# Writing the diagonal blocks of the linear attention's weights into its matrix by one masked copy

## The chip, the cores and the metric

The kernel runs on one core of one Trainium2 chip. The metric is the device time of the program in microseconds (us); lower is better. Its engines are TensorE (PE, matrix products; its weight loads have their own row, PEld), VectorE (DVE), ScalarE (ACT), GpSimd (POOL) and SyncE (SP), each with a queue of its own that it works off in order.

## What is computed

A network of two blocks over 256 tokens and a context of 256. The first block is run for two layers, the second for two. The change touches one branch of the first block, the gated linear attention, in both of its layers and in both directions of time. Its core in the reference, cut:

```python
GLA_HEADS, GLA_DK, GLA_DV, GLA_CHUNK = 4, 64, 128, 64

def gla_scan(q, k, v, g, s0):
    mask = jnp.tril(jnp.ones((GLA_CHUNK, GLA_CHUNK), dtype=bool))
    def step(s, inp):
        qc, kc, vc, gc = inp
        b = jnp.cumsum(gc, axis=2)
        b_last = b[:, :, -1:, :]
        inter = jnp.einsum('bhtd,bhde->bhte', qc * jnp.exp(b), s)
        rel = jnp.where(mask[:, :, None], b[:, :, :, None, :] - b[:, :, None, :, :], -jnp.inf)
        att = jnp.einsum('bhtd,bhsd,bhtsd->bhts', qc, kc, jnp.exp(rel))
        o = inter + jnp.einsum('bhts,bhse->bhte', att, vc)
        s_new = jnp.exp(b_last[:, :, 0, :])[..., None] * s + \
            jnp.einsum('bhsd,bhse->bhde', kc * jnp.exp(b_last - b), vc)
        return s_new, o
    ...
    y_gla = gla_finish(ol_f + flip(ol_b), p['gla_o_norm'], x.dtype) * jax.nn.silu(g_g)
```

`att` is the matrix of weights: for a pair of positions s and t the product of key and query with a decay per channel, exp(b_t - b_s). `o` is `att` times the values plus what the state `s` of earlier chunks gives. The scan runs forward and backward in time, over the context and then over the tokens, and the branch is the sum of both directions.

## The kernel before

`first_block` runs `trunk(0)` for 512 positions (context and tokens, four tiles of 128) and `trunk(1)` for the 256 tokens (two tiles). In each, `gla(l, hp)` is called for two pairs of heads, so the loop over `self.tiles` at L947 has 4 + 4 + 2 + 2 = 12 turns; a turn is called a tile below. Forward and backward channels of a head share the 128 partitions (0 to 63 and 64 to 127), so one product with all of them gives the sum of both directions.

A tile's matrix `att` (128 x 128 for each of two heads) is built by levels, because exp(b_t - b_s) does not factor safely over long distances. At level `lev` a pair of positions in neighbouring blocks of size B = 2^lev is taken by way of the border between them: `e` is the distance of the summed decay `cv` from the border (L972), Abs and Exp on ACT (L974, L975), `qe = e * q` (L977, DVE), half of it set to zero by POOL (L982, L983), `e * k` (L984), and then products of `e` and `qe`. Levels 5 and 6 (blocks of 32 and 64) go straight to their places in the PSUM tile `pa` (L996). Levels 0 to 4 lie inside diagonal blocks of 32; `blocks` (L958) computes for each the four 32x32 diagonal blocks of both heads into `pc[:, lev]` (8 products, L962), 128 partitions x 2 x 32. The plain product of keys and queries (s = t, no decay) goes to `pc[:, 5]`. DVE copies `pc[:, 5]` to `blk` (L999) and puts each level in with `copy_predicated` under a mask of the pairs that belong to it (L1002, five times).

The diagonal blocks of `pa` get products of zeros (`self.zero`, L1006), ACT copies `pa` to `att` (L1007), and the output `po` of each head sums S times `ec` (the state's part, L1014), `att` times `v` (L1015) and, for the diagonal blocks, `blk` times `v` in four products on 32 x 32 parts of the array (L1018). Products of the helper `mm` carry its line, L218, in the trace. In the trace a product of f32 operands shows as two records, and PSUM tiles of this part are called px, those of the big products pg.

Around it: the same PE queue carries the big products of the other branches with weights streamed from memory. `weight` (L237) loads a 512 KB piece by SP's queue (`raw`, three buffers), ACT writes its rounded part `wh` (L214) and DVE the rest `wl` (L215); products then run in three passes (`mm3`). `trunk` steps generators (`units`) for the other branches between the stages of `gla` by fixed paces. The order on each engine is set by the framework's scheduler, which places instructions by its own estimates and by priorities (`urgent`), so an edit in one line can move others. At the end of layer 1, `out_ln` loads rows by POOL's queue: `nwrow`, `wab` (L1238) and two rows into the buffer of `m` (L1068, L1069), which must wait until that buffer's last readers are done.

Of the kernel before, what the change touches and what calls it, by code (L numbers as in the profile page):

```python
# [11 lines left out]
U8 = mybir.dt.uint8  # L12
# [5 lines left out]
P = 128  # L18
# [14 lines left out]
def plan():  # L33
# [9 lines left out]
    for l in range(2):  # L43
# [31 lines left out]
        att()  # L75
        sgu()
        gla(0)
        branch("bs", M_S)
        gate(A_G)
        gla(1)  # L80
        branch("ba", M_A)
        gate(G_G)
# [98 lines left out]
class Builder:  # L181
# [144 lines left out]
    def build(self):  # L326
        nc, tc, io = self.nc, self.tc, self.io
        self.filler = iter(())
        with tc.tile_pool(name="const", bufs=1) as cp, \
# [19 lines left out]
            self.U1, self.L1, self.ones = (con[:, i * P:(i + 1) * P] for i in range(3))  # L349
            self.id32 = con[:, 3 * P:]  # L350
            self.maskc = cp.tile([P, 5, 2, 32], U8, name="maskc")
            self.mask = cp.tile([P, 5, 32], U8, name="mask")

            self.pick = cp.tile([P, 35], F32, name="pick")
            nc.vector.memset(self.pick, 0.0)
            nc.vector.memset(self.pick[:, 2:3], 1.0)
            self.zero = self.pick[:, 3:35]
            self.cols = cp.tile([P, NCOL], F32, name="cols")
            self.rope = cp.tile([P, 2, 2, 64], F32, name="rope")
            self.eps = cp.tile([P, 1], F32, name="eps")  # L360
# [484 lines left out]
    def gla(self, l, hp):  # L845

        nc, tc, io = self.nc, self.tc, self.io
        T0, TN = self.T0, self.TN
        nt = len(self.tiles)
        with tc.tile_pool(name=f"gla{l}{hp}", bufs=1, reuse_waits="tile") as gp:  # L850
# [13 lines left out]
            v = self.t(gp, [P, 4, 256], tag="v")  # L864
# [4 lines left out]
            q = self.t(gp, [P, 2, TN], tag="q")  # L869
# [24 lines left out]
            for i2 in range(2):  # L894
                pc = self.ps()
                for h in range(2):
                    for i in range(2):
                        o = (h * 2 + i) * P
# [14 lines left out]
            for i2 in range(2):  # L913
# [7 lines left out]
                for i in range(2):  # L921
                    for h in range(2):
                        o = (i * 2 + h) * P
# [4 lines left out]
                for i in range(2):  # L928
                    for h in range(2):
                        o = (i * 2 + h) * P  # L930
                        self.mm(pu[:, o:o + P], kt[:, o:o + P], v[:, 2 * i2 + i, h * P:(h + 1) * P], True, True)
                nc.scalar.copy(up[:, 2 * i2:2 * i2 + 2].rearrange("p a b c -> p (a b c)"), pu)
            for (rows, order) in ((slice(0, 64), (0, 1, 2, 3)), (slice(64, 128), (1, 0, 3, 2))):
                nc.gpsimd.memset(S[rows, order[0]], 0.0)
                nc.scalar.copy(S[rows, order[1]], up[rows, order[0]])
                for n in (1, 2):
                    i, nx = order[n], order[n + 1]
# [9 lines left out]
            for n, i in enumerate(self.tiles):  # L947
                tt = i * P - T0
                cv = c[:, :, i * P:(i + 1) * P]
                qv = q[:, :, tt:tt + P]  # L950
                kv = kd[:, :, i * P:(i + 1) * P]

                att = self.t(gp, [P, 2, P], tag="att", bufs=2)
                blk = self.t(gp, [P, 2, 32], tag="blk", bufs=2)
                pc = self.ps()[:, :384].rearrange("p (l a t) -> p l a t", l=6, a=2)
                pa = self.ps()[:, :256].rearrange("p (a t) -> p a t", a=2)

                def blocks(out, x, y):  # L958
                    for a in range(2):
                        for b in range(4):  # L960
                            o = slice(32 * b, 32 * b + 32)
                            nc.tensor.matmul(out[o, a, :], x[:, a, o], y[:, a, o], start=True, stop=True, tile_position=(0, 32 * b))  # L962

                blocks(pc[:, 5], kv, qv)
                for levs in (range(0, 4), range(4, 7)):
                    nl = len(levs)
                    e = self.t(gp, [P, nl, 2, P], tag="e", bufs=2)
# [17 lines left out]
                    for li, lev in enumerate(levs):  # L985
# [5 lines left out]
                        for a in range(2):  # L991
                            for m in range(P // (2 * B)):
                                for d in range(2):
# [2 lines left out]
                                    nc.tensor.matmul(pa[ks, a, ts], e[ch, li, a, ks], qe[ch, li, a, ts], start=True, stop=True,  # L996
                                                     tile_position=(64 * d, s0))
                    if levs[0] == 0:
                        nc.vector.tensor_copy(blk, pc[:, 5])  # L999
                    for lev in levs:  # L1000
                        if lev < 5:
                            nc.vector.copy_predicated(blk, self.mask[:, lev, None, :].to_broadcast([P, 2, 32]), pc[:, lev])  # L1002
                for a in range(2):
                    for b in range(4):
                        o = slice(32 * b, 32 * b + 32)
                        nc.tensor.matmul(pa[o, a, o], self.zero, self.zero, start=True, stop=True, tile_position=(0, 32 * b))  # L1006
                nc.scalar.copy(att, pa)  # L1007
                ec = self.t(gp, [P, 2, P], tag="ec")
                nc.scalar.activation(ec, cv, AF.Exp)
                nc.vector.tensor_tensor(ec, ec, qv, ALU.mult)  # L1010
                po = self.ps()
                for h in range(2):
                    o = po[:, h * P:(h + 1) * P]
                    self.mm(o, ec[:, h, :], S[:, i, h, :], True, False)  # L1014
                    self.mm(o, att[:, h, :], v[:, i, h * P:(h + 1) * P], False, False)  # L1015
                    for b in range(4):
                        r = slice(32 * b, 32 * b + 32)
                        nc.tensor.matmul(o[r], blk[r, h, :], v[r, i, h * P:(h + 1) * P], start=False, stop=True, tile_position=(32 * b, 32 * b))  # L1018
                nc.scalar.copy(oraw[:, n].rearrange("p a b -> p (a b)"), po[:, :256])
                sq = self.t(gp, [P, 2, P], tag="sq")  # L1020
                nc.scalar.activation(sq.rearrange("p a b -> p (a b)"), po[:, :256], AF.Square)
# [786 lines left out]
def lay_out(inp):  # L1808
# [6 lines left out]
    a = {"W": W}  # L1815
# [60 lines left out]
    r = np.arange(P)  # L1876
    le = (r[:, None] <= r[None, :]).astype(np.float32)
    a["con"] = np.concatenate([le, le.T, np.ones((P, P), np.float32), np.tile(np.eye(32, dtype=np.float32), (4, 1))], axis=1)
    q, s = (r % 32)[:, None], np.arange(32)[None, :]
    maskc = np.zeros((P, 5, 2, 32), np.float32)  # L1880
    mask = np.zeros((P, 5, 32), np.float32)
    for lev in range(5):
        mask[:, lev] = ((q >> lev) ^ (s >> lev)) == 1
        maskc[:, lev, 0] = (((q >> lev) ^ (s >> lev)) == 1) & (q < s)
        maskc[:, lev, 1] = (((q >> lev) ^ (s >> lev)) == 1) & (q > s)
    a["mask"] = mask
    a["maskc"] = maskc
    pos = np.arange(256)
# [25 lines left out]
```

## Time and profile before

| | us |
|---|---|
| median of 3 runs | 1463.87 |
| lowest and highest | 1460.82, 1464.85 |
| the profiled execution, its own time | 1456.51 |
| its span in the trace | 1454.8 |
| PE, DVE, ACT busy in the span | 1375.5, 1061.0, 831.6 |

A profile is one execution. The page gives the busy time of each engine and its costliest groups; "windows" give busy time in chosen stretches (us from the span's start); the chain of waits goes back from the last instruction, at each step to what released it; a timeline lists instructions by their starts. The twelve tiles lie between 281 and 340 us (layer 0, first call), 430 and 480 (layer 0, second call), 781 and 815, and 880 and 900 (layer 1).

### The profile page before, as it was taken

How to read it: one execution, taken by the hardware profiler on the slowest of the kernel's cores; microseconds unless marked ns; L12 is line 12 of the kernel's file. 1: busy time of each engine (PE TensorE's matmuls, PEld its weight loads, DVE VectorE, ACT ScalarE, POOL GpSimd, SP SyncE). 2: the span in 40 equal slices, each digit the busy share in tenths (PEclk: the TensorE clock that was granted, in tenths of full speed). 3: DMA queues.
4: the chain of work that ended last, by engine and by line, in shares of the span. 5: the costliest groups of instructions: out<-in, count | busy, mean ns of one | idle time of the engine just before them, and what ended most of it. 6: DMA issues, size and time to landing. Idle time of an engine off the chain costs nothing.

```text
span 1454.8 us, 32364 instructions
## 1 busy us (share of the span) xinstructions
PE 1375.5 (95%) x13420; PEld 1210.5 (83%) x13420; DVE 1061.0 (73%) x2033; ACT 831.6 (57%) x1490; POOL 88.8 (6%) x260
## 2 busy tenths in 40 slices
PE   7898999999999999999999999979899999999998
PEld 4796777877877779997799999879789998989997
DVE  2698895585268248878738648886999776799785
ACT  2435543653275333656567475469695657977654
POOL 0100001010001000110000001011000000100000
PEclk9999999999999999999999999999999999999999
DMA  9552334212211236343234434624323553433362
GB/s 377 200 173 102 131 124 161 84 63 75 91 70 62 85 101 197 127 133 100 91 106 142 143 122 141 202 67 138 119 89 131 162 187 107 131 100 118 116 205 86
DMA packets 52850, 187.55 MB, mean 129 GB/s; under 512 B 6136, under 2 KB 7468, under 8 KB 52704
## 3 DMA queue, kind: packets, MB, share of 16 engines
q1 hardware_dynamic: 44640, 159.85, 32.8%
q0 software_dynamic: 6912, 24.39, 5.1%
q8 instruction: 105, 1.72, 0.5%
q10 hardware_dynamic: 1152, 1.25, 0.3%
q14 instruction: 41, 0.34, 0.1%
HBM read 184.42 MB, written 1.05 MB: 127 GB/s over the span
## 4 chain that ended last, share of the span: by engine, by line
PE 66%; DVE 12%; ACT 11%; issue 5%; DMA 5%; POOL 0%; SPq 0%; DVEq 0%; ACTq 0%; POOLq 0%
PE pg L218 51%; PE px L218 7%; DVE wl L215 3%; ACT wh L214 3%; PE px L227 3%; DMA raw<-in_W 2%; DVE u L1776 2%; DMA adaw<-in_W 1%; PE px L812 1%; PE px L962 1%; PE pa L431 1%; PE px L1018 1%; PE px L996 1%; ACT L1503 1%; DVE hTl L215 1%
## 5 line engine op out<-in xcount | busy, mean ns | idle before, releaser
L215 DVE TENSOR_TENSOR wl<-raw,wh 128x1024 fp32r<-128x1024 f32 x276 | 336.9, 1224 | 192.7 <-ACT wh L214 173.6
L218 PE MATMUL pg<-hTh,wh 128*128 128x256 f32 (+1 forms) x1440 | 455.2, 317 | 1.6 <-issue 1.6
L214 ACT CAST wh<-raw 128x1024 fp32r<-128x1024 f32 (+1 forms) x278 | 289.1, 1043 | 282.7 <-PE pg L218 216.9
L218 PE MATMUL pg<-hTl,wh 128*128 128x256 f32 (+1 forms) x1440 | 449.0, 312 | 0.5 <-DVE ss L726 0.5
L218 PE MATMUL pg<-hTh,wl 128*128 128x256 f32 (+1 forms) x1424 | 444.0, 312 | 0.7 <-DVE wl L215 0.7
L218 PEld LDWEIGHTS pg<-hTh,wh 128*128 128x128 f32 x1440 | 271.2, 188 | 20.5 <-issue 3.9
L218 PEld LDWEIGHTS pg<-hTl,wh 128*128 128x128 f32 x1440 | 271.0, 188 | 19.6 <-issue 4.8
L218 PEld LDWEIGHTS pg<-hTh,wl 128*128 128x128 f32 x1424 | 268.7, 189 | 16.5 <-issue 1.2
L1776 DVE SCALAR_TENSOR_TENSOR u<-cpad,cols,u 128x256 f32<-128x256 f32 x240 | 104.5, 480 | 0.9
L218 PE MATMUL pg<-big,wh 128*128 128x512 f32 (+1 forms) x384 | 99.3, 346 | 3.4 <-DVE big L215 0.9
L218 PE MATMUL pg<-wl,hTh 128*128 128x256 f32 x320 | 91.2, 286 | 2.8 <-DVE wl L215 2.8
L218 PE MATMUL pg<-wh,hTh 128*128 128x256 f32 x320 | 91.5, 286 | 0.3 <-ACT kd L863 0.3
L218 PE MATMUL pg<-wh,hTl 128*128 128x256 f32 x320 | 91.7, 287 | 0.0
L218 PEld LDWEIGHTS pg<-big,wh 128*128 128x128 f32 x384 | 66.5, 191 | 14.4 <-DVE big L215 1.6
L218 PE MATMUL pg<-wh,mh 128*128 128x256 f32 x272 | 76.9, 284 | 0.1
L218 PE MATMUL pg<-wl,mh 128*128 128x256 f32 x272 | 76.6, 283 | 0.3 <-DVE wl L215 0.3
L218 PE MATMUL pg<-wh,ml 128*128 128x256 f32 x272 | 76.7, 282 | 0.0
L218 PE MATMUL pg<-big,wl 128*128 128x512 f32 (+1 forms) x192 | 66.2, 345 | 0.0
L218 PEld LDWEIGHTS pg<-wl,hTh 128*128 128x128 f32 x320 | 61.4, 192 | 3.0 <-DVE wl L215 3.0
L218 PEld LDWEIGHTS pg<-wh,hTl 128*128 128x128 f32 x320 | 61.7, 193 | 1.0 <-issue 0.8
L218 PEld LDWEIGHTS pg<-wh,hTh 128*128 128x128 f32 x320 | 61.5, 192 | 0.7 <-ACT kd L863 0.5
L218 PEld LDWEIGHTS pg<-wh,mh 128*128 128x128 f32 x272 | 51.6, 190 | 0.7 <-issue 0.5
(462 smaller groups left out, 2472.9 us busy)
## 6 DMA issues: line engine op xcount, KB each, us to landing
raw<-in_W SPq DMA_DIRECT2D x282, 512.0 KB, 3.5
adaw<-in_W POOLq DMA_DIRECT2D x32, 512.0 KB, 3.8
araw<-in_W SPq DMA_DIRECT2D x16, 512.0 KB, 9.0
xT<-in_xT SPq DMA_DIRECT2D x4, 512.0 KB, 9.3
yg<-in_xtok POOLq DMA_DIRECT2D x2, 512.0 KB, 4.4
m<-in_xtok POOLq DMA_DIRECT2D x2, 512.0 KB, 6.2
nwrow<-in_nwrow POOLq DMA_DIRECT2D x2, 512.0 KB, 3.8
wsT<-in_sguw POOLq DMA_DIRECT2D x2, 256.0 KB, 3.6
```

The source lines that it names most:

```text
L214: self.nc.scalar.copy(h, src)
L215: self.nc.vector.tensor_tensor(l, src, h.bitcast(F32), ALU.subtract)
L218: self.last_mm = self.nc.tensor.matmul(out, lhsT, rhs, start=start, stop=stop).ins
L227: self.nc.tensor.transpose(out, in_, self.ident[:k, :k])
L431: nc.tensor.matmul(ps[32 * g:32 * g + 32, :P], self.sc[:, k, :], raw[:, o:o + P], start=k == 0, stop=k == 7, tile_position=(0, 32 * g))
L812: nc.tensor.matmul(pv[64 * j:64 * j + 64, :256], kv[kt][:, 128 + 64 * g:192 + 64 * g], pTs[b][:, j * 256:(j + 1) * 256], start=kt == 0, st ...
L962: nc.tensor.matmul(out[o, a, :], x[:, a, o], y[:, a, o], start=True, stop=True, tile_position=(0, 32 * b))
L996: nc.tensor.matmul(pa[ks, a, ts], e[ch, li, a, ks], qe[ch, li, a, ts], start=True, stop=True, tile_position=(64 * d, s0))
L1018: nc.tensor.matmul(o[r], blk[r, h, :], v[r, i, h * P:(h + 1) * P], start=False, stop=True, tile_position=(32 * b, 32 * b))
L1503: nc.scalar.activation(sq, sq, AF.Exp, scale=-0.5)
L1776: nc.vector.scalar_tensor_tensor(out, src, w, out, ALU.mult, ALU.add)
```

## The change

The masks of levels 1 to 4 stay, level 0 needs none: `blk` starts as a copy of level 0, and the later levels are put over it. Four more masks say, for each of the four diagonal blocks, which pairs off the main diagonal belong to it. The product of keys and queries goes to the diagonal blocks of `pa`, where the products of zeros stood, so ACT's copy brings the main diagonal into `att`; then one `copy_predicated` on DVE puts `blk`, read four times over, into the four diagonal blocks of `att` for both heads (256 columns). The output is then S times `ec` and `att` times `v` alone.

```diff
-            self.mask = cp.tile([P, 5, 32], U8, name="mask")
+            self.mask = cp.tile([P, 8, 32], U8, name="mask")
...
-            self.zero = self.pick[:, 3:35]
...
-                pc = self.ps()[:, :384].rearrange("p (l a t) -> p l a t", l=6, a=2)
+                pc = self.ps()[:, :320].rearrange("p (l a t) -> p l a t", l=5, a=2)
...
-                blocks(pc[:, 5], kv, qv)
...
                     if levs[0] == 0:
-                        nc.vector.tensor_copy(blk, pc[:, 5])
+                        nc.vector.tensor_copy(blk, pc[:, 0])
                     for lev in levs:
-                        if lev < 5:
-                            nc.vector.copy_predicated(blk, self.mask[:, lev, None, :].to_broadcast([P, 2, 32]), pc[:, lev])
+                        if 0 < lev < 5:
+                            nc.vector.copy_predicated(blk, self.mask[:, lev - 1, None, :].to_broadcast([P, 2, 32]), pc[:, lev])
                 for a in range(2):
                     for b in range(4):
                         o = slice(32 * b, 32 * b + 32)
-                        nc.tensor.matmul(pa[o, a, o], self.zero, self.zero, start=True, stop=True, tile_position=(0, 32 * b))
+                        nc.tensor.matmul(pa[o, a, o], kv[:, a, o], qv[:, a, o], start=True, stop=True, tile_position=(0, 32 * b))
                 nc.scalar.copy(att, pa)
+                nc.vector.copy_predicated(att.rearrange("p a (b t) -> p a b t", b=4), self.mask[:, None, 4:8].to_broadcast([P, 2, 4, 32]),
+                                          blk[:, :, None, :].to_broadcast([P, 2, 4, 32]))
...
                     self.mm(o, ec[:, h, :], S[:, i, h, :], True, False)
-                    self.mm(o, att[:, h, :], v[:, i, h * P:(h + 1) * P], False, False)
-                    for b in range(4):
-                        r = slice(32 * b, 32 * b + 32)
-                        nc.tensor.matmul(o[r], blk[r, h, :], v[r, i, h * P:(h + 1) * P], start=False, stop=True, tile_position=(32 * b, 32 * b))
+                    self.mm(o, att[:, h, :], v[:, i, h * P:(h + 1) * P], False, True)
...
-    mask = np.zeros((P, 5, 32), np.float32)
+    mask = np.zeros((P, 8, 32), np.float32)
     for lev in range(5):
-        mask[:, lev] = ((q >> lev) ^ (s >> lev)) == 1
+        if lev:
+            mask[:, lev - 1] = ((q >> lev) ^ (s >> lev)) == 1
...
+    for b in range(4):
+        mask[:, 4 + b] = (q != s) & (r // 32 == b)[:, None]
```

The scheduler orders the instructions anew. PE at the output of the first tile (layer 0, first call), before; px_2721 is this tile's `po`, px_2740 the next tile's `pc`, pg a big product:

```order
L218 MATMUL px_2721<-S_2549,ec_2718 128x128 [waits PE_49]
L962 MATMUL px_2740<-q_2477,kd_2324 32x32 [waits PE_49]
L962 MATMUL px_2740<-q_2477,kd_2324 32x32 x7
L218 MATMUL px_2721<-v_2360,att_2610 128x128 [waits Activation_49]
L1018 MATMUL px_2721<-v_2360,blk_2611 32x128 [waits DVE_49]
L1018 MATMUL px_2721<-v_2360,blk_2611 32x128 x3
L218 MATMUL px_2721<-S_2549,ec_2718 128x128
L218 MATMUL px_2721<-v_2360,att_2610 128x128
L1018 MATMUL px_2721<-v_2360,blk_2611 32x128 x4
L218 MATMUL pg_3275<-hTh_102,wl_3272 128x512
L218 MATMUL pg_3275<-hTh_102,wh_3271 128x512
```

and in the changed kernel, where px_2713 is `po`:

```order
L1004 MATMUL px_2613<-q_2477,kd_2324 32x32 x6
L218 MATMUL px_2713<-S_2549,ec_2710 128x128 [waits PE_49]
L218 MATMUL pg_3211<-hTh_102,wl_3208 128x512
L218 MATMUL pg_3211<-hTh_102,wh_3207 128x512
L218 MATMUL pg_3211<-hTl_103,wh_3207 128x512
L218 MATMUL pg_3211<-hTh_102,wl_3208 128x512
L218 MATMUL px_2713<-v_2360,att_2610 128x128 [waits DVE_49]
L218 MATMUL px_2713<-S_2549,ec_2710 128x128
L218 MATMUL px_2713<-v_2360,att_2610 128x128
L218 MATMUL pg_3238<-big_1792,wh_3201 128x512
```

The products with `blk` and the next tile's group of q and kd are gone, four big products stand between S times `ec` and `att` times `v`, and the latter waits for DVE instead of ACT.

DVE at the same tile, before; e is the next tile's distance from the border, and of the lines L1002 the last is level 4:

```order
L1002 COPY_PREDICATED blk_2611<-mask,px_2612 128x64 [waits DVE_49]
L972 TENSOR_TENSOR e_2750<-c_2528 128x256 x2
L1002 COPY_PREDICATED blk_2611<-mask,px_2612 128x64 [waits DVE_49,PE_49]
L972 TENSOR_TENSOR e_2750<-c_2528 128x256
L972 TENSOR_TENSOR e_2805<-c_2528 128x256 x3
L1010 TENSOR_TENSOR ec_2846<-ec_2846,q_2477 128x256 [waits Activation_49]
L1022 TENSOR_REDUCE ss_2609<-sq_2735 128x2 [waits Activation_49]
L977 TENSOR_TENSOR qe_2757<-e_2750,q_2477 128x1024 [waits DVE_49,Activation_49,Pool_49]
```

and in the changed kernel, where L1006 is the masked copy (most of its lines are one to three smaller than before's):

```order
L1000 COPY_PREDICATED blk_2611<-mask,px_2612 128x64 [waits DVE_49]
L970 TENSOR_TENSOR e_2726<-c_2528 128x256 x2
L1000 COPY_PREDICATED blk_2611<-mask,px_2612 128x64 [waits DVE_49,PE_49]
L970 TENSOR_TENSOR e_2726<-c_2528 128x256
L1006 COPY_PREDICATED att_2610<-mask,blk_2611 128x256 [waits DVE_49,Activation_49]
L970 TENSOR_TENSOR e_2780<-c_2528 128x256 x3
L215 TENSOR_TENSOR wl_3304<-raw_3301,wh_3303 128x1024 [waits DMAHW2_49,PE_49,Activation_49]
L1019 TENSOR_REDUCE ss_2609<-sq_2719 128x2 [waits Activation_49]
L658 SCALAR_TENSOR_TENSOR m_418_2101<-th_3236,pg_3238 128x512 [waits PE_49]
L975 TENSOR_TENSOR qe_2733<-e_2726,q_2477 128x1024 [waits DVE_49,Activation_49,Pool_49]
```

The masked copy stands behind level 4 and a subtraction for the next tile, and in front of three more and a split of weights.

POOL at the end of layer 1, before:

```order
L1244 DMA nwrow_10104<-in_nwrow 128x1024 [waits PE_49,Activation_49]
L1238 DMA wab_10111<-in_wab 128x256
L1068 DMA m_1600_10061<-in_postg 128x1024 [waits DMASW3_49,DVE_49,Activation_49]
L1069 DMA m_1600_10061<-in_postb 128x1024
L1238 DMA wab_13667<-in_wab 128x256 [waits DMASW2_49,DMASW5_49,DVE_49,Activation_49]
```

and in the changed kernel:

```order
L1241 DMA nwrow_9912<-in_nwrow 128x1024 [waits PE_49,Activation_49]
L1065 DMA m_1600_9869<-in_postg 128x1024 [waits DVE_49,Activation_49]
L1066 DMA m_1600_9869<-in_postb 128x1024 [waits DMASW3_49]
L1235 DMA wab_9919<-in_wab 128x256
L1235 DMA wab_13475<-in_wab 128x256 [waits DMASW4_49,DMASW5_49,DVE_49,Activation_49]
```

The first load of `wab` has moved behind the two loads into `m`.

## Rows read from the trace of the kernel before

**Rows 1.** The page: busy time by engine, and the split on DVE.

```profile
PE 1375.5 (95%) x13420; PEld 1210.5 (83%) x13420; DVE 1061.0 (73%) x2033; ACT 831.6 (57%) x1490; POOL 88.8 (6%) x260
...
L215 DVE TENSOR_TENSOR wl<-raw,wh 128x1024 fp32r<-128x1024 f32 x276 | 336.9, 1224 | 192.7 <-ACT wh L214 173.6
```

**Rows 2.** Windows: stretch, length, busy (records) by engine, granted clock, DMA.

```profile
270.00:340.00 70.00, 70.00 (x890) 53.56 (x887) 53.86 (x108) 40.30 (x68) 9.34 (x43) 1.00 0.19 63
...
430.00:480.00 50.00, 49.79 (x699) 36.83 (x697) 39.38 (x88) 23.91 (x38) 6.50 (x32) 1.00 0.19 64
...
775.00:815.00 40.00, 39.39 (x569) 36.25 (x569) 33.34 (x71) 22.91 (x42) 4.25 (x19) 1.00 0.40 135
```

**Rows 3.** Chain of waits, 430 to 480: shares, then start, length, what.

```profile
by line: PE pg L218 57.4%; PE px L218 11.4%; PE px L962 8.0%; PE px L1018 5.7%; PE px L996 5.1%; DVE ab L1029 2.5%; PE px L1006 2.1%; issue 1.4%; DVE nw_b L263 1.1%; PE px L227 1.0%; DVE nw_a L262 1.0%; DVE ss L1022 0.9%; ACT sq L1021 0.8%;
...
447.29 0.35 PE px L1018 x8
447.65 0.64 PE px L218 x4
```

**Rows 4.** Single lines, whole span: shortest, median, longest ns, starts, shapes.

```profile
L1018 PE MATMUL px<-v,blk x192: 267/280/293, 293.0 to 899.1; 32*32 32x128 f32 x192
...
L1002 DVE COPY_PREDICATED blk<-mask,px x60: 221/225/235, 288.5 to 897.5; 128x64 f32<-128x64 uint8 x60
...
L972 DVE TENSOR_TENSOR e<-c x84: 417/419/426, 273.7 to 886.6; 128x256 f32<-128x256 f32 x84
```

**Rows 5.** Chain of waits, 775 to 800: four products of v and kt.

```profile
775.09 1.04 PE px L218 x8
```

**Rows 6.** Timeline, PE: the group of q and kd followed by another, and alone.

```profile
782.06 0.33 PE L962 MATMUL px<-q,kd 128*32 128x32 f32 x16
782.21 0.75 PE L962 MATMUL px<-qe,e 128*32 128x32 f32 x64
...
882.75 0.33 PE L962 MATMUL px<-q,kd 128*32 128x32 f32 x16
883.01 0.49 PE L218 MATMUL px<-v,att 128*128 128x128 f32 x2
```

**Rows 7.** Timeline of one tile of layer 0: start, length, instruction, idle before.

```profile
445.14 0.33 PE L1006 MATMUL px<-pick 128*32 128x32 f32 x16
...
445.54 0.37 ACT L1007 COPY att<-px 128x256 f32<-128x256 f32 x1 [6.00 <-PE px L1006]
...
448.57 0.50 PE L218 MATMUL pg<-hTh,wh 128*128 128x512 f32 x1
...
448.90 0.39 PE L218 MATMUL pg<-hTl,wh 128*128 128x512 f32 x1
449.14 0.39 PE L218 MATMUL pg<-hTh,wl 128*128 128x512 f32 x1
```

**Rows 8.** What PE waited for before L1018, whole span: us, times.

```profile
  DVE blk L1002: 0.6, 2
```

**Rows 9.** Timelines of POOL and ACT at the end of layer 1.

```profile
899.95 0.55 POOL L1238 DMA_DIRECT2D wab<-in_wab  x1
912.69 0.53 POOL L1068 DMA_DIRECT2D m<-in_postg  x1 [12.18 <-issue]
...
921.36 0.71 ACT L214 CAST mh<-m 128x256 fp32r<-128x256 f32 x2
```

**Rows 10.** DMA issues: count, size of one, median us to landing.

```profile
wab<-in_wab POOLq DMA_DIRECT2D x2, 128.0 KB, 4.5
...
mask<-in_mask SPq DMA_DIRECT2D x1, 80.0 KB, 7.2
```

**Rows 11.** Chain of waits, end of layer 1: a load of weights.

```profile
914.12 6.25 DMA raw<-in_W
```

**Rows 12.** Windows as in rows 2, at the end of layer 0.

```profile
614.00:616.00 2.00, 0.94 (x5) 0.95 (x6) 1.92 (x5) 1.29 (x3) 0.00 (x0) 0.81 0.13 53
616.00:618.00 2.00, 2.00 (x12) 2.00 (x11) 1.05 (x4) 1.41 (x4) 1.04 (x1) 0.50 0.00 0
618.00:620.00 2.00, 2.00 (x16) 2.00 (x16) 1.73 (x4) 1.69 (x4) 2.00 (x2) 0.83 0.00 0
```

## Prediction

> **What bounds the kernel now.** I read the page first, then the stretches that hold the linear attention, then the chain of waits in them, then single lines. The page says that TensorE (PE) is busy for 95% of the span and VectorE (DVE) for 73% [rows 1]. The twelve tiles that the change touches (four in each of two calls in layer 0, two in each of two calls in layer 1) lie in four stretches; in the three shown PE is busy for 70.0 of 70, 49.8 of 50 and 39.4 of 40 us at a granted clock of 1.00, while DVE has 16, 11 and 7 us free [rows 2]. The chain of waits says the same: in 430 to 480 us nearly all of it down to the last tile's tail is PE, with L218 (the helper of all big products) at 57.4 + 11.4%, L962 at 8.0% and L1018, the line that falls away, at 5.7% [rows 3]. So what PE no longer does there is time saved, as long as nothing makes PE wait instead. A busy PE is not always at its peak, so I price PE work by the distance from one start to the next.
>
> **The products with blk (removed).** Each product of L1018 is two records, 192 in all [rows 4], so 24 groups of 8. On the chain a group takes 0.35 us [rows 3]: 24 x 0.35 = 8.4 us. Between the two groups of a tile stand two 128x128 products (S with ec, v with att) that take 0.64 us [rows 3]; four such products in a row, with no 32x32 groups around them, take 1.04, so two take 0.52 [rows 5]. That is 0.12 more per tile, 1.4 us.
>
> Rule and row differ here. The Trainium skill ("TensorE: Matmul & The Clock Gate", Part 3, Measured speedup vs the span model) says that products on different 32x32 tiles of the array overlap, each further one costing about 4 ns. With the row's 280 ns for one record [rows 4] an estimate by that page is 0.28 + 7 x 0.004 = 0.31 us for a group and 7.4 us for the 24, a gain smaller by 1.0 us. That speaks a little against the change; I stay with the 0.35 that the chain shows.
>
> **The q times k blocks (moved).** The eight 32-column products into pc[:, 5] (16 records) go. They are now written straight into pa's diagonal, where eight products of zeros of the same shape stood, so that place costs the same. The group that goes takes 0.26 us where it stands alone and 0.15 where another such group follows at once [rows 6]. The order shows the second at the first tile of the four calls: 4 x 0.15 + 8 x 0.26 = 2.7 us. At the other eight it lay between S-ec and att, where PE would have had to wait for ACT's copy of att, so its worth could be nothing there (0.6 in all).
>
> The removal is thus 8.4 + 1.4 + 2.7 = 12.5 us; its ends are 10.4 and, if some further changes between the two kinds of product go too, 14.4.
>
> **What PE gets instead.** The order puts big products between S-ec and v-att of every tile. The first big product after a 32x32 group takes 0.33 us to the next start, the second 0.24 [rows 7], so such a switch costs 0.09. Before, seven of the twelve tiles already had big products between att and blk; five more switches are 0.5 us (ends 0 and 1.1).
>
> **DVE.** Per tile one predicated copy of 64 columns goes (0.225 us) and one of 256 comes. No row shows a predicated copy of that size: it lies between 0.225 and four times that, 0.90; the nearest row is a 256-column DVE instruction of 0.419 [rows 4], which I take. DVE gets 12 x 0.2 = 2.3 us more; the free 16, 11 and 7 us of [rows 2] hide them while PE is the bound. ACT does the same instructions.
>
> **The new wait.** v-att waited for ACT's copy of att; now it waits for DVE's masked copy behind that. All big products of the stream queue behind the waiting product. From the start of the diagonal group (445.14) to the start of ACT's copy are 0.40 us, the copy takes 0.37 [rows 7], then DVE 0.42, and a hand-over of 0.14 as from the group's end to ACT: 1.3 to 1.4 us. PE meanwhile does the group (0.26), S-ec (0.26) and what the order puts there: four big products at the first tile (4 x 0.24 + 0.09 = 1.05), 1.57 in all, so it is covered by 0.2 us; a 256-column subtraction that still runs on DVE (0.42) would leave 0.2 open. At the other tiles three to fourteen products stand there. Bounds: nothing, or per tile a whole split (1.22 us, [rows 1]) in front of the copy plus the copy, 1.64, 19.7 us in all. The nearest row is the wait for blk, also a DVE result wanted by PE a little after the same place: 0.6 us in all twelve tiles [rows 8]. I take twice that, 1.2 us.
>
> **Queues that it moves past.** On POOL's queue the first wab load now stands behind the two loads into m. Before, wab was issued at 899.95 and m at 912.69, when its readers were done [rows 9]. Now wab starts about 913.8 and lands 4.5 us later [rows 10] if nothing delays it, say 918 to 921; ACT casts it, by its new order, after the third cast of mh, which ended about 922 [rows 9]. That is just in time: 0 to 3 us, I take 0.4. The mask's load grows from 80 to 128 KB [rows 10] ahead of weights at the start: 0 to 0.3, I take 0.1. The rest of the code after the last tile keeps its order.
>
> **Sum.** -12.5 + 0.5 + 1.2 + 0.4 + 0.1 = -10.3 us. The profiled execution took 1456.5 us (span 1454.8), so 1446.2; the median of the runs, 1463.9, is 0.5% above the profiled one, and the same share there gives 1453.5.
>
> **Rival A, slower: the copy comes late.** DVE takes instructions in order, and a split of weights (1.22 us) may stand in front of the masked copy; at the fourth tile the order has one and a 512-column product there. If that happened at every tile without more cover than today's, PE would lose 12 x 1.64 = 19.7 us: 1456.5 - 12.5 + 1.0 + 19.7 = 1464.7, on the median 1472. It decides from 1.0 us of waiting per tile, where the gain is gone. Against it: the filled place before v-att, and the 0.6 us of [rows 8]. 9%.
>
> **Rival B, no change: given back later.** At the end of layer 1 the chain is loads of weights (6.25 us of it at 914 [rows 11]). If these keep their time, the gain of layer 1's four tiles (4.2 us) is lost, and with 2.6 us for wab: -10.3 + 4.2 + 2.6 = -3.5, on the median 1460.3. Against it: a load starts when a buffer is freed by work that also moves forward. 16%.
>
> **Rival C, slower: the clock.** After a stretch in which PE was idle for half of the time the granted clock was 0.50 and then 0.83 in two stretches of 2 us [rows 12]: 1.0 + 0.3 us lost per fall. If each new wait led to one: 12 x 1.3 = 16, on the median 1469. The Trainium skill ("TensorE: Matmul & The Clock Gate", Why this matters for your kernels) says that idle gaps between bursts of products bring the clock back to half. By the sum above a wait is a few tenths of a us in a stream that shows 1.00 [rows 2]. 2%.
>
> **How the numbers follow.** The forecast, 1453.5, has 73%. A measurement of this kernel tells some 0.3% (4.4 us) from no change: below 1459.5 is faster, above 1468.3 slower. The forecast is faster, B the same, A and C slower: 73, 16 and 11%. The low end takes the removal at 14.4 and no wait (1442.3, on the median 1449.6) less 1.6 for the spread of the runs: 1448. The high end, 1464, is no gain at all; it holds B and leaves out A, C and a little of both ends.
>
> **What would show it.** Right: no line for products with blk, 384 PE records fewer; the chain in the four stretches still PE, the first to the second tile shorter by about 0.9 us; the masked copy at about 0.42 us; PE's wait for it below 0.3 us a tile. Wrong: a wait of v-att for DVE of 1 us and more (A), an ACT wait for wab or later loads at 910 to 930 (B), a granted clock below 1.00 between 270 and 480 (C).

## The result, and the profile after

The changed kernel takes 1445.53 us (median of 4 runs, 1443.17 to 1453.14), the kernel before beside it 1462.38 (4 runs, 1460.82 to 1464.85); the medians differ by 16.9 us. The ratio of the runs is 0.9897, with a 95% interval of 0.987 to 0.9925: 15.1 us (11.0 to 19.0) faster. The forecast was 1453.5 with a range from 1448 to 1464: the direction was right, the gain half as large again as forecast, and the time lies below the range. One thing is needed to read the two profiles: that of before is of an execution shorter than the four timed ones (1456.5), that of after of the longest of its four (1453.1; mean granted clock 0.983 against 0.989), so the spans differ by only 3.6 us; the stretches compared below are therefore bounded by the same big products in both traces, and in layer 0 all of them show a granted clock of 1.00.

The page of after, busy time by engine. TensorE has 384 records fewer than in [rows 1] (192 of blk and v, 192 of q and k), and VectorE is busy for 1.0 us more:

```profile
PE 1365.2 (94%) x13036; PEld 1208.4 (83%) x13036; DVE 1062.0 (73%) x2033; ACT 832.0 (57%) x1490; POOL 88.5 (6%) x260
```

Windows of after over those of [rows 2] (same columns). In the first two PE is the bound as before, with fewer records in the same time; in the third it is now idle for 1.8 us:

```profile
270.00:340.00 70.00, 69.66 (x788) 55.11 (x787) 57.64 (x112) 43.93 (x72) 9.30 (x43) 1.00 0.21 70
430.00:480.00 50.00, 49.80 (x563) 39.09 (x564) 38.81 (x82) 25.27 (x41) 6.11 (x30) 1.00 0.20 65
775.00:815.00 40.00, 38.24 (x515) 36.22 (x514) 33.63 (x75) 20.42 (x34) 3.58 (x15) 1.00 0.42 137
```

The chain of waits of after, 430 to 480 us, by line, and two pieces. It answers to [rows 3]: the 5.7% of L1018 and the groups of products in front of and behind it are gone, and in place of 0.35 + 0.64 + 0.35 us there are six records (three products: v-att, S-ec, v-att) in 0.67:

```profile
by line: PE pg L218 59.8%; PE px L218 7.1%; DVE qe L975 4.4%; issue 3.8%; PE px L961 3.0%; DVE e L970 2.8%; PE px L994 2.5%; DVE wl L215 2.5%; PE px L227 2.1%; ACT wh L214 2.1%; ACT e L972 2.1%; ACT e L973 1.9%; POOL qe L981 1.7%; POOL qe L
...
432.49 0.67 PE px L218 x6
```

The timeline of PE in a tile of after that answers to [rows 7] (L994 levels 5 and 6, L1004 the q k blocks in the diagonal, L961 levels 0 to 4). Nothing of 32 columns stands any more between v-att, S-ec and v-att:

```profile
441.79 0.71 PE L994 MATMUL px<-qe,e 64*32 64x32 f32 x24
442.42 0.33 PE L1004 MATMUL px<-q,kd 128*32 128x32 f32 x16
442.69 0.49 PE L218 MATMUL px<-S,ec 128*128 128x128 f32 x2
442.93 0.71 PE L218 MATMUL pg<-big,wh 128*128 128x512 f32 x2
443.48 0.39 PE L218 MATMUL pg<-big,wl 128*128 128x512 f32 x1
443.80 0.33 PE L961 MATMUL px<-qe,e 128*32 128x32 f32 x16
...
446.25 0.48 PE L218 MATMUL px<-v,att 128*128 128x128 f32 x2
446.57 0.39 PE L218 MATMUL px<-S,ec 128*128 128x128 f32 x2
446.79 0.39 PE L218 MATMUL px<-v,att 128*128 128x128 f32 x2
446.94 0.48 PE L218 MATMUL pg<-hTh,wh 128*128 128x512 f32 x1
```

Of the masked copy (L1006) the trace of after gives, over the whole span, shortest, median and longest ns, and who waited for it. It answers to [rows 8]:

```profile
L1006 DVE COPY_PREDICATED att<-mask,blk x12: 443/450/458, 295.4 to 893.9; 128x256 f32<-128x256 uint8 x12
...
  PEld px L218: 0.8, 3
```

**Where the time came from.** Both traces hold 7292 records of big products by L218, in layer 0 in the same sequence (in layer 1, 37 places of it hold another product). Windows between the same two places, first of before, over the four tiles of the first call of layer 0, the four of the second, and the last two tiles with the end of layer 1 (two windows):

```profile
281.09:361.22 80.13, 80.07 (x911) 61.46 (x909) 57.91 (x117) 37.94 (x60) 9.34 (x43) 1.00 0.21 68
430.18:545.13 114.95, 113.48 (x973) 87.52 (x972) 62.07 (x114) 46.61 (x70) 7.55 (x34) 1.00 0.25 82
...
866.05:900.03 33.98, 33.48 (x519) 30.19 (x518) 27.95 (x53) 23.47 (x41) 4.72 (x22) 1.00 0.42 136
900.03:930.24 30.21, 26.81 (x194) 24.49 (x192) 26.30 (x62) 16.36 (x28) 2.07 (x4) 0.94 0.60 208
```

and the same work in after:

```profile
283.98:358.09 74.11, 74.00 (x782) 58.67 (x781) 58.61 (x117) 37.20 (x60) 9.30 (x43) 1.00 0.22 73
426.73:535.76 109.03, 107.44 (x860) 84.55 (x859) 63.14 (x115) 46.59 (x70) 7.56 (x34) 1.00 0.27 87
...
857.17:887.79 30.62, 28.37 (x391) 26.93 (x390) 25.09 (x46) 21.77 (x37) 3.70 (x18) 1.00 0.41 136
887.79:921.19 33.40, 28.18 (x259) 27.03 (x257) 27.94 (x67) 17.97 (x32) 2.53 (x6) 0.90 0.57 192
```

Layer 0 gains 6.0 + 5.9 = 11.9 us, 1.5 a tile (the prediction had 0.9), and TensorE is busy for all but 0.1 and 1.6 us of the two stretches, as it was before. The first call of layer 1 gains 1.9 (74.21 to 72.33, from the starts of the products that bound it). The second gains 3.4 and gives 3.2 of them back at once. With 0.3 between the calls of layer 0 that is 14.3 us in this pair of traces, within the interval of the times. The trace of after loses 11 us outside of these stretches (3 ahead of the first tile, 2 between layer 0's tiles and layer 1's, 6 behind layer 1); by the two mean clocks an estimated 9 us in the whole span went to time at half clock.

### The profile page after: what moved, and what is told of

It is laid out like the page before. It is cut to its first block, busy times and chain, and to the rows that moved or that the text cites. A ratio compares the mean times of both kernels' runs of the same rounds, so it can differ in the third digit from the quotient of the medians.

```text
span 1451.2 us, 31609 instructions
## 1 busy us (share of the span) xinstructions
PE 1365.2 (94%) x13036; PEld 1208.4 (83%) x13036; DVE 1062.0 (73%) x2033; ACT 832.0 (57%) x1490; POOL 88.5 (6%) x260
## 4 chain that ended last, share of the span: by engine, by line
PE 64%; DVE 14%; ACT 12%; issue 5%; DMA 5%; POOL 1%; SPq 0%; ACTq 0%; DVEq 0%; POOLq 0%
PE pg L218 49%; PE px L218 7%; DVE wl L215 4%; ACT wh L214 3%; PE px L227 3%; DVE u L1773 2%; DMA raw<-in_W 2%; DMA adaw<-in_W 2%; PE px L811 1%; PE pa L430 1%; DVE hTl L215 1%; PE px L961 1%; ACT L1500 1%; ACT q L874 1%; PE px L994 1%
## 5 line engine op out<-in xcount | busy, mean ns | idle before, releaser
L218 PE MATMUL pg<-hTh,wh 128*128 128x256 f32 (+1 forms) x1440 | 457.4, 318 | 1.2 <-issue 0.6
L218 PE MATMUL pg<-hTl,wh 128*128 128x256 f32 (+1 forms) x1440 | 451.4, 314 | 2.8 <-issue 2.0
L218 PE MATMUL pg<-hTh,wl 128*128 128x256 f32 (+1 forms) x1424 | 445.6, 313 | 0.8 <-DVE wl L215 0.8
L218 PEld LDWEIGHTS pg<-hTh,wh 128*128 128x128 f32 x1440 | 272.9, 190 | 21.7 <-issue 4.2
L218 PEld LDWEIGHTS pg<-hTl,wh 128*128 128x128 f32 x1440 | 272.7, 189 | 17.4 <-issue 2.1
L218 PEld LDWEIGHTS pg<-hTh,wl 128*128 128x128 f32 x1424 | 270.5, 190 | 18.0 <-issue 2.7
L218 PE MATMUL pg<-big,wh 128*128 128x512 f32 (+1 forms) x384 | 99.3, 347 | 5.5 <-DVE th L619 3.0
L218 PE MATMUL pg<-wl,hTh 128*128 128x256 f32 x320 | 91.0, 285 | 2.9 <-DVE wl L215 2.9
L218 PE MATMUL pg<-wh,hTh 128*128 128x256 f32 x320 | 91.0, 285 | 0.3 <-ACT kd L862 0.3
L218 PE MATMUL pg<-wh,hTl 128*128 128x256 f32 x320 | 91.2, 285 | 0.0
L218 PEld LDWEIGHTS pg<-big,wh 128*128 128x128 f32 x384 | 66.6, 194 | 14.7 <-DVE th L619 3.6
L218 PE MATMUL pg<-wh,mh 128*128 128x256 f32 x272 | 76.8, 284 | 1.0 <-DVE ot L1101 0.4
L218 PE MATMUL pg<-wl,mh 128*128 128x256 f32 x272 | 76.7, 283 | 0.3 <-DVE wl L215 0.3
L218 PE MATMUL pg<-wh,ml 128*128 128x256 f32 x272 | 76.6, 282 | 0.0
L218 PE MATMUL pg<-big,wl 128*128 128x512 f32 (+1 forms) x192 | 66.4, 347 | 0.0
L218 PEld LDWEIGHTS pg<-wl,hTh 128*128 128x128 f32 x320 | 60.8, 190 | 3.3 <-DVE wl L215 3.3
L218 PEld LDWEIGHTS pg<-wh,hTl 128*128 128x128 f32 x320 | 61.0, 191 | 1.4 <-issue 1.2
L218 PEld LDWEIGHTS pg<-wh,hTh 128*128 128x128 f32 x320 | 61.0, 191 | 0.7 <-ACT kd L862 0.5
L218 PEld LDWEIGHTS pg<-wh,mh 128*128 128x128 f32 x272 | 51.6, 190 | 1.7 <-ACT wh L214 0.9
```

Of the source, the lines that this page charges most:

```text
L218: self.last_mm = self.nc.tensor.matmul(out, lhsT, rhs, start=start, stop=stop).ins
```

## Experiments: what the removed products cost

The theory formed from the result: TensorE pays at every change between products on the whole array (128x128, or 512 columns) and products on a part of it (32 or 64 wide), in both directions. Counting the linear attention's own small products, the order of instructions has 138 such changes in the kernel before and 56 in the changed one. The rival is the prediction's own price. Three parts of the change or of its reverse, each alone:

**b_noblk**, the kernel before without the products of blk and v:

```
-  self.mm(o, att[:, h, :], v[:, i, h*P:(h+1)*P], False, False)
-  for b in range(4): ... matmul(o[r], blk[r, h, :], v[r, i, ...], start=False, stop=True, ...)
+  self.mm(o, att[:, h, :], v[:, i, h*P:(h+1)*P], False, True)
```

> The kernel before without the 24 groups of products of blk and v; everything else stays, so the diagonal blocks of the weights are built but never reach the output. Theory (edges): a group of 32x32 products costs more than its own 0.35 us, because the 128x128 or 512-column product in front of it takes about 0.42 instead of 0.24 us to the next start, and the one behind it 0.33 instead of 0.24. Then the two groups of a tile and the two products between them cost 0.70 + 0.18 + 0.09 + 0.09 + 0.08 = 1.14 us, and twelve tiles become 13.7 us faster: 1448.7 on the median of 1462.4. Rival (own time): the groups are worth what the prediction gave them, 8.4 + 1.4 = 9.8 us, so 1452.6, and the rest of the gain of 16.9 us came from elsewhere (the q k blocks, the order of the instructions).

Measured: 1446.89 us, ratio 0.9896 (0.987 to 0.9922), 11.4 to 19.0 us faster; the rival's 9.8 lies outside.

**b_blklast**, the kernel before with both groups of a tile in one row behind its last full product:

```
   for h in range(2):
     S-ec, v-att (now with stop=True)
+  for h in range(2):
+    o = po[:, 256 + h*P:256 + (h+1)*P]
     for b in range(4): ... matmul(o[r], blk[r, h, :], v[r, i, ...], start=True, stop=True, ...)
```

> The kernel before with the same products, but both groups of blk and v of a tile stand in one row behind all four 128x128 products, and write to the free half of the PSUM tile, so that the diagonal blocks are left out of the output. The number of products is that of the kernel before; a tile has one group between full products instead of two. Edges: one product in front of a group (0.18) and one behind it (0.09) fewer per tile, and the second group in a row costs less than 0.35 (0.15 where two groups of q and k stood in a row): 12 x 0.27 = 3.2 up to 12 x 0.47 = 5.6 us faster, 1457 to 1459. Own time: 12 x 0.12 = 1.4 us faster at most, 1461.

Measured: 1456.85 us, ratio 0.9959 (0.9942 to 0.9975), 3.7 to 8.5 us faster with the same number of products; the rival's 1.4 lies outside. PE's timeline of a tile (L1020 are the products of blk and v):

```profile
444.16 0.49 PE L218 MATMUL px<-v,att 128*128 128x128 f32 x2
444.49 0.39 PE L218 MATMUL px<-S,ec 128*128 128x128 f32 x2
444.71 0.39 PE L218 MATMUL px<-v,att 128*128 128x128 f32 x2
445.03 0.64 PE L1020 MATMUL px<-v,blk 32*32 32x128 f32 x16
445.60 0.33 PE L962 MATMUL px<-q,kd 128*32 128x32 f32 x14
```

By the distance of starts S-ec costs 0.22 us here where full products stand on both sides of it, and v-att 0.32 where a group follows. Both groups together take 0.57; in the kernel before it was 0.35 for each. So the second one in a row adds 0.22.

**b_qk**, the kernel before with only the q k blocks moved into the diagonal of the PSUM tile:

```
-  blocks(pc[:, 5], kv, qv)
-  nc.vector.tensor_copy(blk, pc[:, 5])
+  nc.vector.tensor_copy(blk, self.zero[:, None, :].to_broadcast([P, 2, 32]))
-  matmul(pa[o, a, o], self.zero, self.zero, ...)
+  matmul(pa[o, a, o], kv[:, a, o], qv[:, a, o], ...)
```

> The kernel before with only the q times k blocks moved into the diagonal of the PSUM tile (in the place of the products of zeros); blk starts from zeros instead of their copy, the products of blk and v stay, and the diagonal q k terms arrive by att. The output is that of the reference. Own time: 4 x 0.15 + 8 x 0.26 = 2.7 us faster, 1459.7. Edges: where the group stood alone between big products it also cost 0.27 at its neighbours, 8 x 0.27 = 2.2 more, so 4.9 us faster, 1457.5.

In this kernel the other pairs of the diagonal blocks get their product without decay besides the right one, which the expectation overlooked; the instructions are as it says. Measured: 1449.64 us, ratio 0.9918 (0.9886 to 0.995), 7 to 17 us faster. That is more than either theory said. Its trace gains 4.0 us in layer 0's two stretches and 1.4 and 1.8 in the two calls of layer 1, 7.2 in all, the low end of that interval; the rest of the 12 us by the times is not shown to come from the tiles.

**a_row and a_alt**, the changed kernel with the same extra work in two orders:

```
   v-att of the second head
+  for _ in range(6): full()       # a_row          + for _ in range(6):   # a_alt
+  for _ in range(6): group()                      +     full(); group()
```

> The changed kernel with extra work at the end of each tile, whose results nobody reads: six 128x128 products in a row, then six groups of four 32x32 products in a row. The order of TensorE's instructions shows 24 more changes between products on the whole array and products on a part of it than in the changed kernel (80 instead of 56). It is the base for the run a_alt: 72 products of 0.24 us and 72 groups of 0.31 us or less would make it 30 to 42 us slower than the changed kernel, about 1480.

> The same extra work as in a_row, but product and group take turns: 200 changes of kind instead of 80, nothing else differs. Edges: each change costs about 0.09 us (0.42 - 0.33 in front of a group, 0.33 - 0.24 behind one), so 120 x 0.09 = 10.8 us slower than a_row. Own time: only a product that stands between two groups is dearer, by the 0.06 us a piece that the prediction took (0.12 for two), 60 x 0.06 = 3.6 us.

Measured: 1480.43 (1477.33 to 1484.57) and 1495.46 us (1493.29 to 1496.24): the order alone costs 15.0 us by the medians. PE's timeline of the first tile of a_row, then the big product that follows; twelve records (six products) take 1.43 us to the next start and 48 records (six groups) 1.44. Each of the two rows ends with a change; by the single starts inside them a product or a group takes 0.22:

```profile
294.10 1.50 PE L218 MATMUL px<-q,kd 128*128 128x128 f32 x12
295.53 1.51 PE L1021 MATMUL px<-v 32*32 32x128 f32 x48
296.97 0.73 PE L218 MATMUL pg<-big,wh 128*128 128x512 f32 x2
```

and of the same tile in a_alt, where each product takes 0.42 and each group 0.35:

```profile
296.13 0.49 PE L218 MATMUL px<-q,kd 128*128 128x128 f32 x2
296.55 0.42 PE L1021 MATMUL px<-v 32*32 32x128 f32 x8
296.90 0.49 PE L218 MATMUL px<-q,kd 128*128 128x128 f32 x2
297.32 0.42 PE L1021 MATMUL px<-v 32*32 32x128 f32 x8
297.67 0.49 PE L218 MATMUL px<-q,kd 128*128 128x128 f32 x2
```

So two changes cost 0.42 + 0.35 - 2 x 0.22 = 0.33 us, 0.16 each on average. By a_row's single starts the change into the groups costs 0.12 (0.09 in the last full product, 0.02 in the first group) and the one out of them 0.21 (half in the last group, half in the product behind it). What happens at one can be read from the weight loads (PEld) of the kernel before, in the tile of [rows 7]: at three of the four changes the load sits idle for 0.20 to 0.24 us (0.12 at the fourth), into a group and out of one, where between full products (447.79) it starts under the product before it:

```profile
447.22 0.15 PEld L1018 LDWEIGHTS px<-v,blk 32*32 32x32 f32 x8 [0.24 <-issue]
447.57 0.30 PEld L218 LDWEIGHTS px<-S,ec 128*128 128x128 f32 x2 [0.20 <-issue]
447.79 0.30 PEld L218 LDWEIGHTS px<-v,att 128*128 128x128 f32 x2
448.21 0.15 PEld L1018 LDWEIGHTS px<-v,blk 32*32 32x32 f32 x8
448.57 0.19 PEld L218 LDWEIGHTS pg<-hTh,wh 128*128 128x128 f32 x1 [0.20 <-issue]
```

The Trainium skill ("TensorEngine Tiling (Array Packing)", Key Properties) states that a change of the tiling mode drains TensorE. The trace agrees: the loads stop there, and two changes cost 0.33 us.

One price for all. The gain in layer 0's two stretches (lengths between the same big products, clock 1.00 in each), beside what 0.22 us for a group of blk, 0.15 for one of q k [rows 6] and 0.14 for a change would give. The 0.14 is the last row's 11.1 us over its 80 changes:

| kernel | changes there | two stretches, us | gain | by these prices |
|---|---|---|---|---|
| before | 88 | 80.13 + 114.95 | | |
| changed | 36 | 74.11 + 109.03 | 11.9 | 16 x 0.22 + 8 x 0.15 + 52 x 0.14 = 12.0 |
| b_noblk | 52 | 75.34 + 110.24 | 9.5 | 16 x 0.22 + 36 x 0.14 = 8.6 |
| b_blklast | 60 | 78.02 + 112.94 | 4.1 | 28 x 0.14 = 3.9 |
| b_qk | 64 | 78.03 + 113.01 | 4.0 | 8 x 0.15 + 24 x 0.14 = 4.6 |
| a_alt against a_row | 132, 52 | 92.37 + 127.47, 86.95 + 121.76 | -11.1 | 80 x 0.14 = -11.2 |

All agree within 0.9 us. Of the nearly 2 us by which the 80 changes cost less than at the 0.16 of the single starts, 1.1 was idle time of TensorE that the longer work filled (2.7 us in a_row's two stretches, 1.6 in a_alt's); the rest isn't explained. The expectations had 0.09, from single starts, and so a_alt's 10.8 us for all twelve tiles was too low (11.1 in layer 0's eight alone): they took the 0.35 of a lone group for its own time, of which 0.13 belongs to its changes.

## Experiments: the copy, and the end of layer 1

**a_nocopy and a_copy4**, the changed kernel with no masked copy and with four:

```
-  nc.vector.copy_predicated(att..., self.mask[:, None, 4:8]..., blk...)     # a_nocopy: gone; a_copy4: four times
```

> The changed kernel without the masked copy: the off-diagonal part of the diagonal blocks is left out of the output. PE waited 0.8 us for the copy in all of the profiled execution. If the copy costs what the profile shows, this is 0 to 1 us faster than the changed kernel: 1444.7 to 1445.5. Rival: the copy costs more than PE's visible wait, because the 0.45 us on DVE push twelve times the splits of weights behind it: 12 x 0.45 = 5.4 us faster, 1440.

> The changed kernel with the masked copy four times in a row instead of once (the same result each time): 36 more of 0.45 us, 16.2 us of DVE. The order puts more big products between S-ec and v-att than in the changed kernel (nineteen instead of nine at the second tile). If DVE time at this place is hidden as the prediction's middle value had it, the kernel is 0 to 3 us slower than the changed one. If v-att waits for DVE as in rival A, it is up to 16 us slower, 1461.

Measured: 1446.55 us (0.9885, 0.9862 to 0.9908) and 1449.73 (0.9918, 0.9887 to 0.9948). In layer 0's two stretches a_nocopy takes 74.37 + 109.05 us and a_copy4 73.67 + 108.66, against 74.11 + 109.03: there neither the copy nor 10.8 us more of it cost anything (a_copy4 has four changes fewer there, worth 0.6). Of the 4 us by which its median lies above that of the changed kernel its trace shows 3.1 in the last call's two windows (67.09 against 64.02).

**l1_pe, l1_dve and p1** asked what sets the time of the last call, where the gain was given back. A first reading was that VectorE and the weight loads behind it bound that stretch, since a_row's extra products in it had cost next to nothing.

```
+  for _ in range(8): full()   then   for _ in range(8): group()     # l1_pe, only where l == 1 and hp == 1
+  for _ in range(10): nc.vector.copy_predicated(att...)              # l1_dve, there
+  (nc.gpsimd if lev >= 4 else nc.vector).tensor_tensor(dst, ...)     # p1, there
```

> The changed kernel with extra TensorE work in the last two tiles alone (second call of layer 1): eight 128x128 products and eight groups of 32x32 products in a row at the end of each, read by nobody. By the rows of a_row (1.43 and 1.44 us for six) that is 2 x 3.8 + 2 x 0.14 x 2 = 8.2 us of TensorE. Theory (DVE and the loads it releases bound the stretch from 866 to 930 us): 0 to 3 us slower than the changed kernel, and what is lost up to 900 comes back up to 930. Rival (TensorE bounds it, as in layer 0): 8 us slower.

> The changed kernel with the masked copy of the last two tiles done ten times in a row (the same result each time): 18 more of 0.45 us, 8.1 us of DVE in the second call of layer 1. Theory (DVE bounds that stretch): the splits of weights behind the copies come later, and with them the loads into the buffers that they free: 6 to 9 us slower than the changed kernel. Rival (TensorE bounds it): 0 to 3 us, as for the copies of a_copy4 in layer 0, which cost nothing there.

> The changed kernel with three of the seven subtractions of cv (levels 4 to 6) of the last two tiles on POOL instead of DVE: 6 x 0.42 = 2.5 us less DVE in the stretch that the theory holds for bound by DVE. If so, up to 2.5 us faster than the changed kernel; slower by the difference where POOL's subtraction takes much longer than DVE's and the stage behind it waits, 0 to 4 us.

Measured: 1451.58 us (0.9937, 0.9914 to 0.996), 1456.29 (0.9969, 0.9953 to 0.9985) and 1448.0 (0.9917, 0.9898 to 0.9937). The windows of l1_pe that answer to the last two of after above:

```profile
853.89:894.77 40.88, 38.59 (x616) 36.08 (x614) 29.61 (x64) 23.05 (x40) 5.21 (x22) 1.00 0.39 130
894.77:925.52 30.75, 25.49 (x195) 23.40 (x193) 25.86 (x51) 17.01 (x29) 1.60 (x3) 1.00 0.55 181
```

They sum to 71.63 us against 64.02: the 8.2 us of TensorE cost 7.6 there, although the granted clock was 1.00 in both windows, so the reading that VectorE and those loads alone bound it fell. Nor does POOL's relief of VectorE gain anything (p1). For l1_dve the two stretches take 74.92. Its trace names who waited for the copies:

```profile
L1007 DVE COPY_PREDICATED att<-mask,blk x30: 439/449/466, 293.6 to 902.2; 128x256 f32<-128x256 uint8 x30
...
  PE px L218: 6.4, 1
```

One v-att waited for 6.4 us: rival A's mechanism, which exists, but needs 4 us more of copies in front of one product. DVE's time isn't free in the last call either: with 0, 1, 4 and 10 copies a tile its two windows take 62.29 (a_nocopy), 64.02, 67.09 and 74.92 us, at a granted clock of 0.95, 0.90, 0.82 and 0.78 in the second one. These are single traces, and two others with one copy a tile take 64.08 (g3) and 65.0 (p1), so the first of these steps is near the scatter. The clock also bears on a_row: 5.7 us of its products in the last call seem to cost nothing (its windows sum to 64.35 us), but both of them show 1.00 where the changed kernel has 0.90 in the second, an estimated 3 us (a tenth of its 33.4). Which engine bounds the last call by itself stays open.

**g1 and g3** tried to go further down the same road, with 48 changes instead of 56:

```
-  for levs in (range(0, 4), range(4, 7)):      # g1 (e in one buffer for each stage)
+  for levs in (range(0, 5), range(5, 7)):
+  with self.behind(self.last_blk):             # g3: levels 5 and 6 issued behind level 4
     nc.tensor.matmul(pa[ks, a, ts], ...)
```

> The changed kernel with levels 0 to 4 in one stage and 5 and 6 in the other (it was 0 to 3 and 4 to 6), with one buffer of e for each stage. The group of level 4 no longer stands alone: 48 changes of kind instead of 56. Edges: 8 x 0.09 = 0.7 us faster than the changed kernel if the longer first stage keeps nobody waiting; a single buffer of e can cost more than that, 1 to 5 us slower.

> The changed kernel in which the products of levels 5 and 6 are issued behind those of level 4 of the same tile, so that all products of the second stage and the q k blocks stand in one row: 48 changes of kind instead of 56, the same instructions on every engine. Edges: 8 x 0.12 to 8 x 0.16 = 1.0 to 1.3 us less TensorE time in the tiles, 1444.3 if nothing gives it back, which the times alone can't tell from the changed kernel; the trace can, by the start of the same big product. Rival: the products of levels 5 and 6 wait for POOL's zeros of level 4 (0.2 us each), with S-ec and v-att queued behind them: no gain or up to 3 us slower.

Measured: 1447.23 us (0.99, 0.9875 to 0.9925) and 1445.49 (0.9885, 0.986 to 0.9911), neither to be told from the changed kernel. In layer 0 g3 takes 73.79 + 108.85 us, 0.5 less than the changed kernel for six changes fewer (0.8 by the price), and g1 72.65 + 108.81, 1.7 less; the last call gives g1's back. No version beats the changed kernel by what can be measured.

## Why the prediction was wrong in size

**The bound was read rightly** for layer 0: what TensorE no longer did there became time saved, 74.00 of 74.11 us busy after as before, and no wait took its place.

**The step that failed is the price of the products next to the removed groups**, "two 128x128 products ... 0.12 more per tile, 1.4 us", together with "five more switches are 0.5 us". It looked only at the two full products between the two groups of blk, and took the groups' 0.35 for their own time. The full product in front of the first group and the one behind the second paid too, and so did the neighbours of each lone q k group. And it counted changes only where a full product follows a group, and took them to grow by five, where the order has 82 fewer. Taken together the terms 8.4, 1.4, 2.7 and -0.5 hold 24 x 0.22 + 12 x 0.15 = 7.1 us of own time and so 4.9 for the changes; at 0.14 they are worth 82 x 0.14 = 11.5. The 0.35 us of [rows 3] was thus right as a sum but was partly the price of a change: in a row a group takes 0.22. The low end of the range let "further changes" add 1.9 us, which is why the time fell below it (1456.5 - 14.4 is 1442.1 and not the text's 1442.3, a slip that changes nothing).

**The q k blocks**, 2.7 us: for layer 0 the sum had 2 x 0.15 + 6 x 0.26 = 1.9, b_qk shows 4.0 there, for the same reason.

**The new wait**, 1.2 us: 0.8 in three tiles, all of layer 0, and a_nocopy shows that it cost nothing there. The cover was as the text had it: at the first tile the copy ended at 295.81 us and v-att started at 296.03, behind four big products, 0.2 us later. The masked copy takes 0.450 us, near the 0.42 taken. That DVE's added time is hidden, too, holds for layer 0 only (above).

**POOL's queue**, 0.4 us: nothing seen. The timeline of POOL in after shows wab behind the loads into m, but these themselves start 7 us earlier than in [rows 9]:

```profile
905.29 0.54 POOL L1065 DMA_DIRECT2D m<-in_postg  x1 [8.92 <-DVE big L215]
905.82 0.53 POOL L1066 DMA_DIRECT2D m<-in_postb  x1
906.34 0.54 POOL L1235 DMA_DIRECT2D wab<-in_wab  x1
```

and ACT casts wab right behind other work, with no idle time in front of it:

```profile
911.57 0.41 ACT L214 CAST mh<-m 128x256 fp32r<-128x256 f32 x1 [0.26 <-DVE m L661]
911.96 0.41 ACT L214 CAST wabs<-wab 128x256 fp32r<-128x256 f32 x1
```

**Rival B** was half right: of layer 1's gain the last call's part didn't arrive (64.19 to 64.02 us over both windows). PE's timeline of after shows where, in two waits for work that hangs on the weights, and the chain of waits still has two loads of weights in it, as before's had (4.29 us at 907.48 and the 6.25 of [rows 11]):

```profile
901.04 0.50 PE L218 MATMUL pg<-big,wh 128*128 128x256 f32 x2 [2.25 <-DVE th L619]
...
904.88 1.04 PE L218 MATMUL pg<-big,wh 128*128 128x256 f32 x3 [2.39 <-ACT big L214]
```

```profile
896.87 4.86 DMA raw<-in_W
...
908.40 4.83 DMA raw<-in_W
```

With them the granted clock of that window fell from 0.94 to 0.90. By the prices above the last call should have given 4 x 0.22 + 2 x 0.15 + 16 x 0.14 = 3.4 us and the first call of layer 1, which gave 1.9, 4 x 0.22 + 2 x 0.15 + 12 x 0.14 = 2.9; the whole change 7.1 + 11.5 = 18.6, without the last call 15.2, against 15.1 measured. That these two agree so closely is partly luck, as the interval is 8 us wide. So one term was too small by 6.6 us, half of that was lost again at a place that the text had named, and the 1.7 us of added costs (1.2, 0.4 and 0.1) were not seen. **Rival A** didn't occur (above). **Rival C** didn't in the tiles of layer 0, where the clock stayed at 1.00; the 0.90 at the end of layer 1 came with the two waits above, and no wait for the copy stands there.

## What to carry to other kernels

Where TensorE is the bound, price a group of small-tile products by two numbers: its own time in a row of its like, and the changes between whole-array and part-array products that go with it, counted over the engine's whole instruction order before and after the edit. The edges lie in the starts of the neighbours on both sides of the group, so compare a stretch between two products that the edit doesn't touch, not the rows of the group alone. A gain in a stretch that ends in a wait for loads counts only as far as the work behind that wait also starts earlier.

## What the runs showed of the hardware

A change between products on the whole array and on a part of it costs time in both directions at a granted clock of 1.00: 0.33 us for the two around a group of 32x32 products by the alternating rows (0.12 into groups, 0.21 out of them in a_row), and 0.14 each, in the length of the stretches, by 80 of them in a_alt against a_row. Six groups of four 32x32 products in a row take 1.44 us, as much as six 128x128 products (1.43). A predicated copy of 256 columns takes 450 ns and one of 64 takes 225 [rows 4], so less than in proportion to its columns.
